# Attention with shared keys: the division by the softmax sums moved from the probabilities to the result

## The chip, the core and the metric

The kernel runs on one core of a Trainium2 chip as one program. The metric is its time on the device in microseconds (us). Five engines work side by side, each with its own queue of instructions that it takes in order: TensorE (PE; its weight loads are shown apart as PEld), VectorE (DVE), ScalarE (ACT), GpSimd (POOL), and SyncE (SP), which here issues all DMA transfers. Engines wait for each other through semaphores.

## The reference, cut to what matters

One layer of an encoder is applied to two requests that share the weights, a long one (1024 tokens) and a short one (512), each with 16 meta tokens ahead. Half of the mixer is grouped-query attention ("group A"): 8 query heads of width 64, four of which share one key and value head.

```
def gqa_block(qblk):
    s = jnp.einsum('bqhgd,bkhd->bhgqk', qblk, ka, preferred_element_type=jnp.float32) * scale
    p = jax.nn.softmax(s, axis=-1).astype(va.dtype)
    return jnp.einsum('bhgqk,bkhd->bqhgd', p, va)
```

`softmax` is exp(s - max) over its own sum along the keys. That division by the sum is what the change moves. The rest of the layer (projections, the differential attention of "group B", the output projection, a gated feed-forward part with a convolution, three norms) is computed as before.

## The kernel before, in words

All products are made in float32 precision: each operand is split into a high and a low part (function `split`, L114 on ACT for the high and L115 on DVE or POOL for the low part), and two or three matmuls are summed.

The program goes through these stages: the projections of the short request (`s = 1`); then the projections of the long request (`s = 0`) merged with the attention of the short one; then the attention of the long request merged with the output projection (`mixer_out`) and the feed-forward part (`conv_glu`) of the short one; then the rest for the long one. `merge` draws work from two generators by the sizes that they yield; behind it the framework's scheduler sets the order of the instructions on each engine, by its own estimate of times, so the order of a whole stage can shift when one operation goes.

Group A works in units: one head and 512 query positions. There are 8 units for the short and 16 for the long request, 24 in all. A unit has four softmaxes of 128 queries each. In `softmax`, scores come from TensorE chunk by chunk (L431, L432), DVE scales them into the tile `p` and takes the chunk's maximum (L433), DVE reduces the maxima (L436, `nm`), ACT makes the exponentials in place and their sum `l` (L438), DVE takes one over the sum (L442, `r`). Then DVE multiplies all of `p` by `r` (L508): 128 x 1040 numbers for the long request, 128 x 528 for the short one. `weighted_v` transposes the four `p` on TensorE, chunk by chunk of the keys (L456), splits the transposed chunk (L114, L115: `pt_hi`, `pt_lo`) and multiplies by the values (L470, L471, and L480 for the last 16 keys). Its result `o` has the output of the values' high parts in rows 0 to 63 and of their low parts in rows 64 to 127; `finish_a` copies the second half (L487, ACT) and adds it (L489, DVE: `o_a`), and SP sends `o_a` to scratch memory (`g.oT`, L514).

Two more things matter. `g.last_rows` holds the last two instructions of a softmax; the first four softmaxes of the long request are issued ahead, and `mixer_out` orders its splits behind those (`g.first_rows`). And SP issues everything in one queue: the loads of `q`, `k`, values and weights (`w_f`, L175), the stores to scratch, and the loads `m` of the attention's results in `mixer_out` (L608, three buffers).

Of the kernel before, what the change touches and what calls it, by code (L numbers as in the profile page):

```python
# [382 lines left out]
def attention(ctx, g, s, side):  # L383
# [40 lines left out]
    def softmax(q, k, inverse=True):  # L424
# [11 lines left out]
        nc.vector.tensor_reduce(out=nm, in_=mx[:, :nch], axis=AX.X, op=ALU.max, negate=True)  # L436
        l = sp.tile([P, 1], F32, name="l", tag="l")[:M]
        g.last_exp = nc.scalar.activation(p, p, AF.Exp, bias=nm, accum_out=l).ins  # L438
# [46 lines left out]
    def finish_a(o, W):  # L485
        low = op.tile([P, 512], F32, name="o_low", tag="w1", bufs=1)[:HD, :W]
        nc.scalar.copy(low, o[HD:P, :])  # L487
        oa = op.tile([P, 512], F32, name="o_a", tag="o")[:HD, :W]
        nc.vector.tensor_tensor(out=oa, in0=o[0:HD, :], in1=low, op=ALU.add)  # L489
        return oa  # L490

    nblk = N // 512
    for kv in range(2):
# [3 lines left out]
        for i in range(4):  # L497
            h = kv * 4 + i
            for b in range(nblk):
                off = 2 if b == 0 else 0  # L500
                q = load_q(QA + h // 2, h % 2, NMETA + 512 * b - off, 512 + off)
                if b == 0:
                    for f in range(2):
                        nc.gpsimd.tensor_copy(halo[f][:, 2 * i:2 * i + 2], q[f].bitcast(F32)[:, 0:2])
                pl = []
                for t in range(4):
                    p, _, r = softmax([x[:, off + t * P:off + (t + 1) * P] for x in q], k)
                    g.last_rows = [g.last_exp, nc.vector.tensor_scalar(  # L508
                        out=p, in0=p, scalar1=r, scalar2=None, op0=ALU.mult).ins]
# [49 lines left out]
    for h in range(4):  # L559
        ks = [load_k(KB + h, m) for m in range(2)]  # L560
        v = load_v(1 + h, 2 * P, 0)
        rows = g.oT[s][512 + h * P:512 + (h + 1) * P]
        for blk in blocks:
# [6 lines left out]
            nc.sync.dma_start(out=rows[:, c1:c1 + W - lead], in_=ob[:, lead:])  # L570
# [685 lines left out]
def trunk_kernel(ctx, tc, g):  # L1256
# [4 lines left out]
    g.qk, g.v, g.vt, g.oT = [], [], [], []  # L1261
    for s, N in enumerate(SEQS):
# [5 lines left out]
        g.oT.append(dram.tile([D, N + 1], F32, name=f"oT{s}"))  # L1268

# [157 lines left out]
```

## Time and profile before

| what | value |
|---|---|
| median of 3 runs | 2134.44 us (2131.06 to 2139.33) |
| the profiled execution: its own time | 2127.9 us |
| its span | 2126.1 us |
| granted TensorE clock, mean | 0.989 |
| PE / PEld busy | 96% / 86% of the span |
| DVE / ACT / POOL busy | 81% / 54% / 26% |

Matmuls are pipelined, so a PE that is shown as busy is not a PE at its peak; PEld and the number of matmuls in a stretch say more. Idle time of an engine costs only where the chain of waits runs through it. "Windows" are stretches of the span with the busy time of each engine in them; "groups" put together instructions of one line and shape. Times in the profile are those of one execution.

### The profile page before, as it was taken

How to read it: one execution, taken by the hardware profiler on the slowest of the kernel's cores; microseconds unless marked ns; L12 is line 12 of the kernel's file. 1: busy time of each engine (PE TensorE's matmuls, PEld its weight loads, DVE VectorE, ACT ScalarE, POOL GpSimd, SP SyncE). 2: the span in 40 equal slices, each digit the busy share in tenths (PEclk: the TensorE clock that was granted, in tenths of full speed). 3: DMA queues.
4: the chain of work that ended last, by engine and by line, in shares of the span. 5: the costliest groups of instructions: out<-in, count | busy, mean ns of one | idle time of the engine just before them, and what ended most of it. 6: DMA issues, size and time to landing. Idle time of an engine off the chain costs nothing.

```text
span 2126.1 us, 35236 instructions
## 1 busy us (share of the span) xinstructions
PE 2040.4 (96%) x12302; PEld 1822.3 (86%) x12302; DVE 1725.0 (81%) x3786; ACT 1156.0 (54%) x2253; POOL 560.8 (26%) x494
## 2 busy tenths in 40 slices
PE   6999999998999999999999999988999999999998
PEld 6988888997887989999989999987887777778877
DVE  6878889767879788888998885578778878879886
ACT  6635566544567556666666765345444444435454
POOL 4653233453112000000000000421544444330112
PEclk9999999999999999999999999999999999999999
DMA  7563435457621322223352225996322232247443
GB/s 255 176 203 130 119 111 171 153 178 236 209 79 56 105 75 67 74 82 118 104 187 88 86 97 147 276 290 217 107 100 90 101 113 84 94 167 260 119 126 127
DMA packets 171426, 296.31 MB, mean 139 GB/s; under 512 B 21456, under 2 KB 90608, under 8 KB 170736
## 3 DMA queue, kind: packets, MB, share of 16 engines
q1 hardware_dynamic: 171248, 294.05, 42.5%
q8 instruction: 97, 1.59, 0.3%
q14 instruction: 81, 0.66, 0.1%
HBM read 211.13 MB, written 82.85 MB: 138 GB/s over the span
## 4 chain that ended last, share of the span: by engine, by line
PE 76%; DVE 12%; DMA 4%; issue 3%; ACT 2%; POOL 1%; SPq 0%; DVEq 0%; ACTq 0%; POOLq 0%
PE ps_mm L121 17%; PE ps_mm L123 17%; PE ps_mm L122 17%; PE ps_t L456 5%; PE ps_s L431 3%; PE ps_s L432 3%; PE ps_s L122 2%; PE ps_s L123 2%; PE ps_s L121 2%; DVE p L433 2%; PE ps_o L471 2%; DVE w_lo L115 1%; PE ps_o L470 1%; DVE acc L972 1%; DMA m<-oT 1%
## 5 line engine op out<-in xcount | busy, mean ns | idle before, releaser
L121 PE MATMUL ps_mm<-xhi,w_hi 128*128 128x258 f32 (+3 forms) x1264 | 383.1, 303 | 12.3 <-ACT xhi L114 5.6
L122 PE MATMUL ps_mm<-xlo,w_hi 128*128 128x258 f32 (+3 forms) x1264 | 378.4, 300 | 0.3 <-POOL xlo L115 0.3
L123 PE MATMUL ps_mm<-xhi,w_lo 128*128 128x258 f32 (+3 forms) x1264 | 377.1, 299 | 0.3 <-DVE w_lo L115 0.3
L433 DVE TENSOR_SCALAR_CACHE_REDUCE p<-ps_s 114x344 f32<-114x344 f32 (+4 forms) x562 | 257.8, 489 | 28.1 <-PE ps_s L432 16.8
L114 ACT CAST pt_hi<-ps_t 128x512 fp32r<-128x512 f32 (+6 forms) x360 | 169.6, 484 | 180.8 <-PE ps_t L456 153.3
L121 PEld LDWEIGHTS ps_mm<-xhi,w_hi 128*128 128x128 f32 x1264 | 239.6, 190 | 18.3 <-ACT xhi L114 7.8
L438 ACT ACTIVATE p<-p,nm 114x1040 f32<-114x1040 f32 (+5 forms) x212 | 214.8, 1013 | 70.5 <-DVE nm L436 69.3
L115 DVE TENSOR_TENSOR w_lo<-w_f,w_hi 128x1024 fp32r<-128x1024 f32 (+1 forms) x182 | 195.2, 1080 | 67.3 <-ACT w_hi L114 66.8
L122 PEld LDWEIGHTS ps_mm<-xlo,w_hi 128*128 128x128 f32 x1264 | 240.0, 190 | 1.9 <-POOL xlo L115 0.8
L123 PEld LDWEIGHTS ps_mm<-xhi,w_lo 128*128 128x128 f32 x1264 | 239.4, 190 | 1.2 <-DVE w_lo L115 0.5
L114 ACT CAST w_hi<-w_f 128x1024 fp32r<-128x1024 f32 (+1 forms) x199 | 167.4, 856 | 79.3 <-PE ps_mm L122 52.2
L115 DVE TENSOR_TENSOR pt_lo<-ps_t,pt_hi 128x512 fp32r<-128x512 f32 (+4 forms) x312 | 172.0, 562 | 42.5 <-ACT pt_hi L114 40.9
L115 POOL TENSOR_TENSOR a_lo<-gate,a_hi 128x256 fp32r<-128x256 f32 x44 | 43.1, 981 | 540.9 <-ACT a_hi L114 521.0
L431 PE MATMUL ps_s<-k,q 128*114 128x348 f32 (+4 forms) x552 | 182.7, 336 | 3.2 <-DVE p L433 3.0
L456 PE MATMUL ps_t<-ident,p 128*128 128x128 f32 (+7 forms) x1188 | 182.4, 269 | 0.9 <-DVE nm L436 0.5
L121 PE MATMUL ps_s<-xhi,w_hi 128*128 128x256 f32 (+4 forms) x480 | 148.2, 311 | 23.2 <-DVE t L333 7.7
L432 PE MATMUL ps_s<-k,q 128*114 128x348 f32 (+4 forms) x552 | 170.3, 313 | 0.0
L456 PEld LDWEIGHTS ps_t<-ident,p 128*128 128x128 f32 (+7 forms) x1188 | 139.9, 135 | 29.1 <-issue 6.8
L123 PE MATMUL ps_s<-xhi,w_lo 128*128 128x256 f32 (+4 forms) x480 | 147.0, 307 | 3.2 <-DMA w_lo<-wo 3.0
L122 PE MATMUL ps_s<-xlo,w_hi 128*128 128x256 f32 (+4 forms) x480 | 148.7, 311 | 1.2 <-DVE xlo L115 0.5
L122 PE MATMUL ps_mm<-t_lo,w_hi 128*128 128x512 f32 (+2 forms) x368 | 142.8, 388 | 1.4 <-DVE t_lo L115 1.4
L121 PE MATMUL ps_mm<-t_hi,w_hi 128*128 128x512 f32 (+2 forms) x368 | 142.8, 388 | 0.0
(273 smaller groups left out, 5269.7 us busy)
## 6 DMA issues: line engine op xcount, KB each, us to landing
w_f<-w_gate SPq DMA_DIRECT2D x46, 512.0 KB, 3.4
w_f<-w_up SPq DMA_DIRECT2D x44, 512.0 KB, 3.3
w_f<-w_in SPq DMA_DIRECT2D x36, 512.0 KB, 4.0
a_f<-act SPq DMA_DIRECT2D x62, 256.0 KB, 2.7
w_f<-w_down SPq DMA_DIRECT2D x22, 512.0 KB, 3.4
act<-a_t SPq DMA_DIRECT2D x44, 256.0 KB, 2.1
a<-w_down SPq DMA_DIRECT2D x40, 256.0 KB, 5.4
w_hi<-wo SPq DMA_DIRECT2D x36, 256.0 KB, 5.2
```

The costliest lines, as they stand in the source:

```text
L114: return (nc.scalar.copy(hi, src).ins, (lo_engine or nc.vector).tensor_tensor(out=lo, in0=src, in1=hi.bitcast(F32), op=ALU.subtract).ins)
L115: (lo_engine or nc.vector).tensor_tensor(out=lo, in0=src, in1=hi.bitcast(F32), op=ALU.subtract).ins)
L121: nc.tensor.matmul(ps, lhsT=whi, rhs=xhi, start=start, stop=False)
L122: nc.tensor.matmul(ps, lhsT=whi, rhs=xlo, start=False, stop=False)
L123: return nc.tensor.matmul(ps, lhsT=wlo, rhs=xhi, start=False, stop=stop).ins
L431: nc.tensor.matmul(ps, lhsT=q[0], rhs=k[:, c0:c0 + cw], start=True, stop=False)
L432: nc.tensor.matmul(ps, lhsT=q[1], rhs=k[:, c0:c0 + cw], start=False, stop=True)
L433: nc.vector.tensor_scalar(out=p[:, c0:c0 + cw], in0=ps, scalar1=HD ** -0.5, scalar2=-3.0e38, op0=ALU.mult, op1=ALU.max, accum_out=mx[:, i: ...
L438: g.last_exp = nc.scalar.activation(p, p, AF.Exp, bias=nm, accum_out=l).ins
L456: nc.tensor.transpose(tps[:, c:c + M], p[:, k0:k0 + kw], g.ident[:M, :M])
L470: nc.tensor.matmul(o, lhsT=v[:, i, :], rhs=hi, start=i == 0, stop=False)
L471: nc.tensor.matmul(o, lhsT=v[:, i, :], rhs=lo, start=False, stop=False)
```

## The change

The values are multiplied by the exponentials as they are, and the result is divided. The sums of the four softmaxes of a unit go to one tile `l4` (128 x 4, two buffers). After the fourth softmax DVE takes one over all four columns at once; SP sends the tile to a row of 512 numbers in scratch memory (one per unit, `g.r`), and loads that row back, repeated on 64 partitions, into half of the tile `rows` (one buffer, whose two halves are used in turn). `finish_a` works in the same half, and GpSimd multiplies its result by `rows` before it is stored. L508 and three of each four reciprocals go. `g.last_rows` now names the maximum's reduction and the exponential, in `softmax` itself. The differential attention and the short "halo" softmaxes of group A keep their way. In the blocks of the differential attention a variable is renamed.

```diff
-    def softmax(q, k, inverse=True):
+    def softmax(q, k, inverse=True, l=None):
...
-        nc.vector.tensor_reduce(out=nm, in_=mx[:, :nch], axis=AX.X, op=ALU.max, negate=True)
-        l = sp.tile([P, 1], F32, name="l", tag="l")[:M]
-        g.last_exp = nc.scalar.activation(p, p, AF.Exp, bias=nm, accum_out=l).ins
+        most = nc.vector.tensor_reduce(out=nm, in_=mx[:, :nch], axis=AX.X, op=ALU.max, negate=True)
+        if l is None:
+            l = sp.tile([P, 1], F32, name="l", tag="l")[:M]
+        g.last_rows = [nc.scalar.activation(p, p, AF.Exp, bias=nm, accum_out=l).ins, most.ins]
...
-    def finish_a(o, W):
-        low = op.tile([P, 512], F32, name="o_low", tag="w1", bufs=1)[:HD, :W]
-        nc.scalar.copy(low, o[HD:P, :])
-        oa = op.tile([P, 512], F32, name="o_a", tag="o")[:HD, :W]
-        nc.vector.tensor_tensor(out=oa, in0=o[0:HD, :], in1=low, op=ALU.add)
+    def finish_a(o, W, half=slice(0, HD)):
+        other = slice(HD - half.start, P - half.start)
+        low = op.tile([P, 512], F32, name="o_low", tag="w1", bufs=1)[half, :W]
+        nc.scalar.copy(low, o[other])
+        oa = op.tile([P, 512], F32, name="o_a", tag="o")[half, :W]
+        nc.vector.tensor_tensor(out=oa, in0=o[half], in1=low, op=ALU.add)
         return oa
...
+    rows = op.tile([P, 512], F32, name="r_rows", tag="r_rows", bufs=1)
...
                 pl = []
+                l4 = sp.tile([P, 4], F32, name="l4", tag="l4", bufs=2)
                 for t in range(4):
-                    p, _, r = softmax([x[:, off + t * P:off + (t + 1) * P] for x in q], k)
-                    g.last_rows = [g.last_exp, nc.vector.tensor_scalar(
-                        out=p, in0=p, scalar1=r, scalar2=None, op0=ALU.mult).ins]
+                    p = softmax([x[:, off + t * P:off + (t + 1) * P] for x in q], k, False, l4[:, t:t + 1])[0]
                     pl.append(p)
+                    if t == 3:
+
+                        nc.vector.reciprocal(out=l4, in_=l4)
+                        row = g.r[s][h * nblk + b]
+                        nc.sync.dma_start(out=row.rearrange("(t p) -> p t", p=P), in_=l4)
+                        c = (h * nblk + b) % 2 * HD
+                        half = slice(c, c + HD)
+                        nc.sync.dma_start(out=rows[half], in_=row.unsqueeze(0).broadcast_to([HD, 512]))
                     yield 2 * n
                 o, W = yield from weighted_v(pl, v, False)
-                oa = finish_a(o, W)
+                oa = finish_a(o, W, half)
+                nc.gpsimd.tensor_tensor(out=oa, in0=oa, in1=rows[half], op=ALU.mult)
                 nc.sync.dma_start(out=g.oT[s][h * HD:(h + 1) * HD, 1 + 512 * b:513 + 512 * b], in_=oa)
...
+        g.r.append([dram.tile([512], F32, name=f"r{s}_{i}") for i in range(8 * N // 512)])
```

The scheduler moves instructions on every engine from the first unit of group A to the end of that attention. Three places are shown; line numbers of the change stand up to 13 higher than those of the kernel before.

DVE where the long request's attention begins, before; `p` and `mx` are a softmax's scores and maxima, `xlo` from `m` the first low parts of `mixer_out`, numbers tell buffers apart:

```order
L436 TENSOR_REDUCE nm_7262<-mx_7249 128x1
L433 TENSOR_SCALAR p_7308,mx_7309<-ps_s_7314 128x348
L442 RECIPROCAL r_6995<-l_6993 128x1
L433 TENSOR_SCALAR p_7308,mx_7309<-ps_s_7318 128x344
L433 TENSOR_SCALAR p_7329,mx_7330<-ps_s_7331 128x348
L508 TENSOR_SCALAR p_6977<-p_6977,r_6995 128x1040
L115 TENSOR_TENSOR xlo_6876<-m_7002,xhi_6875 128x258
```

The same place in the change:

```order
L436 TENSOR_REDUCE nm_7190<-mx_7177 128x1
L433 TENSOR_SCALAR p_7232,mx_7233<-ps_s_7238 128x348
L516 RECIPROCAL l4_6852<-l4_6852 128x4
L433 TENSOR_SCALAR p_7232,mx_7233<-ps_s_7242 128x344
L115 TENSOR_TENSOR xlo_6813<-m_6928,xhi_6812 128x258
```

The scaling is gone from between the chunks of scores, the first low part of `mixer_out` stands one chunk further ahead, and one reciprocal of four columns stands where one of four did.

PE at the change from the long request's projections to its attention, before; `ps_mm` are the projections, `ps_s` the scores:

```order
L121 MATMUL ps_mm_6829<-xhi7_1921,w_hi_6751 128x272
L122 MATMUL ps_mm_6829<-xlo7_1929,w_hi_6751 128x272
L123 MATMUL ps_mm_6829<-xhi7_1921,w_lo_6752 128x272
L431 MATMUL ps_s_6916<-k_6900,q_6908 128x348
L432 MATMUL ps_s_6916<-k_6900,q_6910 128x348
```

And the first scores of that attention in the change:

```order
L123 MATMUL ps_mm_6614<-xhi7_1943,w_lo_6575 128x384
L431 MATMUL ps_s_6855<-k_6838,q_6846 128x348
L432 MATMUL ps_s_6855<-k_6838,q_6848 128x348
L431 MATMUL ps_s_6859<-k_6838,q_6846 128x348
L432 MATMUL ps_s_6859<-k_6838,q_6848 128x348
L431 MATMUL ps_s_6863<-k_6838,q_6846 128x344
L432 MATMUL ps_s_6863<-k_6838,q_6848 128x344
L121 MATMUL ps_mm_6650<-xhi0_1936,w_hi_6574 128x272
```

Before, the last projection's matmul stood right ahead of the first scores. Now the scores of the first softmax stand ahead of the last four chunks of projections (96 matmuls), and part of those of the next among them.

SP in the change, at the long request's first unit; `r0_0` is the row in scratch memory, `r_rows` the tile that it is repeated into, `wo` a store of split weights:

```order
L518 DMA r0_0_80<-l4_6852 128x4x1
L620 DMA m_6941<-oT1_115 128x255
L620 DMA m_6946<-oT1_115 128x258
L620 DMA m_6950<-oT1_115 128x255
L521 DMA r_rows_6837<-r0_0_80 64x512
L630 DMA wo0_125<-w_hi_7002 128x1024
L402 DMA q_7924<-qk0_1_61 128x1x514
```

The row's store and its load are new in this queue; the load waits for the store to land, with stores, queries and weights queued behind it.

More of the change, by code (lines that the diff above doesn't have):

```diff
@@ L561, in attention @@
         v = load_v(1 + h, 2 * P, 0)
-        rows = g.oT[s][512 + h * P:512 + (h + 1) * P]
+        out = g.oT[s][512 + h * P:512 + (h + 1) * P]
         for blk in blocks:
```

4 lines of the change are left out of this document (2 added, 2 removed).

## The prediction

> **What bounds the kernel now.** I read the page first, then the chain of waits by stretches, then the windows of the stretches where group A runs. Two lines of the page: busy time, and the chain that ended last.
>
> ```profile
> PE 2040.4 (96%) x12302; PEld 1822.3 (86%) x12302; DVE 1725.0 (81%) x3786; ACT 1156.0 (54%) x2253; POOL 560.8 (26%) x494
> PE 76%; DVE 12%; DMA 4%; issue 3%; ACT 2%; POOL 1%; SPq 0%; DVEq 0%; ACTq 0%; POOLq 0%
> ```
>
> So TensorE sets the time over most of the span, and DVE over an eighth. What matters is whether the scalings (L508) lie in that eighth. The busy time of L508 alone, by windows that cover all of group A (no scaling runs from 345 to 500 us):
>
> ```profile
> core 0: us, DVE busy (x), PEclk, DMA share, GB/s
> 160.00:190.00 30.00, 5.12 (x8) 0.87 0.46 152
> 190.00:345.00 155.00, 15.62 (x24) 1.00 0.42 126
> 500.00:550.00 50.00, 7.57 (x10) 0.97 0.75 250
> 550.00:620.00 70.00, 8.78 (x11) 1.00 0.46 149
> 620.00:672.00 52.00, 7.07 (x9) 1.00 0.21 59
> 672.00:960.00 288.00, 26.09 (x34) 1.00 0.26 79
> sum 645.00, DVE 70.25; mean DVE 11.71
> ```
>
> All engines in three of them, and in the longest for comparison:
>
> ```profile
> core 0: us, PE busy (x) PEld busy (x) DVE busy (x) ACT busy (x) POOL busy (x), PEclk, DMA share, GB/s
> 160.00:190.00 30.00, 26.01 (x146) 23.61 (x146) 25.95 (x84) 16.05 (x37) 11.70 (x16) 0.87 0.46 152
> 500.00:550.00 50.00, 42.06 (x236) 33.59 (x235) 45.27 (x152) 30.43 (x58) 5.75 (x10) 0.97 0.75 250
> 620.00:672.00 52.00, 46.39 (x265) 35.28 (x264) 51.54 (x154) 37.47 (x76) 14.78 (x21) 1.00 0.21 59
> 672.00:960.00 288.00, 288.00 (x1951) 262.14 (x1951) 238.12 (x629) 174.93 (x293) 21.09 (x24) 1.00 0.26 79
> ```
>
> And the chain of waits in the same four, in order:
>
> ```profile
> by line: DVE p L433 14.5%; DVE p L508 11.4%; DVE t L321 7.6%; PE ps_mm L121 7.0%; PE ps_t L456 5.7%; ACT p L438 5.4%; PE ps_mm L122 5.1%; PE ps_mm L123 5.1%; PE ps_o L471 4.1%; DVE w L273 4.0%; DVE w L274 3.7%; DVE hn L106 3.5%; DVE hn L107
> by line: DMA m<-oT 29.1%; DVE p L433 20.3%; DMA q<-qk 10.8%; issue 5.3%; DVE w_lo L115 4.6%; DVE xlo L115 4.0%; ACT xhi L114 3.1%; PE ps_t L456 2.9%; DVE pt_lo L115 2.5%; PE ps_s L431 2.5%; DVE p L508 2.5%; PE ps_s L432 2.2%; POOL u L275 2.
> by line: DVE p L433 24.2%; DVE pt_lo L115 15.2%; DVE p L508 8.4%; DVE t L761 8.2%; issue 5.7%; DVE pt_hi L115 3.9%; POOL xlo L115 3.4%; ACT pt_hi L114 3.2%; PE ps_t L456 3.0%; DVE w_lo L115 2.8%; DVE o_a L489 2.3%; PE ps_o L470 2.3%; ACT w_
> by line: PE ps_mm L121 18.9%; PE ps_mm L122 18.7%; PE ps_mm L123 18.5%; PE ps_t L456 14.3%; PE ps_s L431 7.5%; PE ps_s L432 7.3%; PE ps_o L471 6.8%; PE ps_o L470 6.5%; PE ps_o L480 1.5%
> ```
>
> From 672 to 960 us the chain never leaves TensorE: the 26.1 us of scalings there cost nothing, and their removal brings nothing. In the three short stretches DVE is the bound: when the short request's first units meet the projections; when the long request's attention starts beside `mixer_out`; and when `conv_glu` normalises its input, where DVE is busy 51.5 of 52 us. What TensorE loses there bounds any gain: at the weight-load share of the longest stretch (262.14 of 288, 0.91) the three would show 27.3, 45.5 and 47.3 us instead of 23.6, 33.6 and 35.3, so 3.7 + 11.9 + 12.0 = 27.6 us.
>
> **What is removed.** All 96 scalings, 70.25 us of DVE, and 72 of 96 reciprocals. The reciprocals in the three stretches:
>
> ```profile
> 160.00:190.00 30.00, 1.32 (x9) 0.87 0.46 152
> 500.00:550.00 50.00, 1.59 (x10) 0.97 0.75 250
> 620.00:672.00 52.00, 1.46 (x10) 1.00 0.21 59
> ```
>
> The chain's own shares of L508 are 0.114 x 30 = 3.4, 0.025 x 50 = 1.3 and 0.084 x 52 = 4.4 us, 9.1 us together: the gain if nothing else moves. If each microsecond of DVE work in the three counted, it would be 5.1 + 7.6 + 7.1 = 19.8 us of scalings and three quarters of 4.4 us of reciprocals, 23 us. I take, stretch by stretch: the first 4 us, its chain share and half of its reciprocals. The last 6 us, between 4.4 and 8.2, since DVE has no gap there but TensorE and ACT take over parts of the chain. The middle one 4 us, between 1.3 and 8.8: four scalings stand in an unbroken run of DVE work ahead of the first low parts of `mixer_out`, and the order now puts the scores of the first softmax ahead of four chunks of projections, so that TensorE has work where it had 236 matmuls in 50 us. In the other three windows I take nothing. The longest is TensorE's alone, and the other two nearly so:
>
> ```profile
> 190.00:345.00 155.00, 151.44 (x971) 136.32 (x970) 133.51 (x428) 94.82 (x223) 47.73 (x42) 1.00 0.42 126
> 550.00:620.00 70.00, 69.98 (x526) 65.98 (x525) 52.58 (x143) 38.48 (x68) 13.07 (x15) 1.00 0.46 149
> ```
>
> Weight loads take 0.88 and 0.94 of them, against 0.91 in the longest. If that cover were gone, they would add at most their 15.6 and 8.8 us of scalings. Sum of the gains: 14 us.
>
> **What is added.** GpSimd multiplies 64 x 512 numbers 24 times. Its nearest groups:
>
> ```profile
> L115 POOL TENSOR_TENSOR a_lo<-gate,a_hi 128x256 fp32r<-128x256 f32 x44 | 43.1, 981 | 540.9 <-ACT a_hi L114 521.0 <-issue 15.7 <-ACT pt_hi L114 2.9
> L910 POOL TENSOR_TENSOR w_s<-w_f 128x512 f32<-128x512 f32 x31 | 52.9, 1707 | 72.7 <-DVE w_lo L115 58.7 <-issue 13.2
> L1017 POOL TENSOR_TENSOR a_t<-act 128x512 f32<-128x512 f32 x22 | 28.4, 1290 | 27.3 <-DMA act<-act 23.6 <-DVE act L1009 3.7
> ```
>
> Half the columns take 0.98 us, as many take 1.29 to 1.71; I take 1.4 us, 34 us in all, beside a GpSimd that is busy 7% to 39% of the windows above. The result's PSUM buffer is free again before the multiply, and its store is needed only in the next stage. Behind the multiply on GpSimd stand the rotary products of the projections in the short request's units, and the low parts `xlo` of `conv_glu` from 620 us on, for which TensorE does wait; there the order puts two multiplies among sixteen splits, up to 2.8 us. I take 1 us.
>
> The row goes out as 512 single numbers and comes back as 64 rows of 2 KB (128 KB). The nearest transfers, with KB each and the median time to landing last:
>
> ```profile
> oT<-o_a SPq DMA_DIRECT2D x16, 0.2 KB, 1.8
> m<-oT SPq DMA_DIRECT2D x8, 0.5 KB, 2.5
> m<-oT SPq DMA_DIRECT2D x8, 172.0 KB, 5.6
> yT<-y SPq DMA_DIRECT2D x32, 128.0 KB, 1.9
> oT<-o_a SPq DMA_DIRECT2D x24, 128.0 KB, 3.0
> ```
>
> 64 numbers land in 1.8 us, 128 in 2.5; the slowest kind of `m` load takes 5.6 (172 KB). I put the row at 3 us (between 1.8 and 5.6) and its load at 3 us (1.9 to 3.4). Their 6 us are hidden if the result comes later. Fourth scaling and result of the long request's first unit, from the timeline:
>
> ```profile
> 517.55 0.76 DVE L508 TENSOR_SCALAR p<-p,r 128x1040 f32<-128x1040 f32 x1
> ...
> 546.64 0.68 DVE L489 TENSOR_TENSOR o_a<-ps_o,o_low 64x512 f32<-64x512 f32 x1
> ```
>
> That is 29 us, so the row waits for the result, not the other way. What isn't hidden is SP: the row's load waits for its store to land, and for those 3 us nothing behind it is issued. In the second stretch the chain runs through such loads in series:
>
> ```profile
> 526.05 7.00 DMA m<-oT
> 533.97 4.48 DMA m<-oT
> 539.42 3.08 DMA m<-oT
> ```
>
> One row's 3 us falls among them with some of it on the path; I take 1 us (nothing to 5.6). The 23 other waits I put at nothing: the transfers behind them are queries, weights and stores that were asked for ahead. If that cover were gone, each would cost 1.8 to 5.6 us.
>
> Net: 14 - 1 - 1 = 12 us less. The profiled execution took 2127.9 us (span 2126.1), so 2115.9. It stands 6.5 us under the median of the runs, 2134.4; the same step gives **2122 us**.
>
> **A rule against it.** The splits of weights on DVE read two operands from SBUF, those of the transposed chunks one from PSUM:
>
> ```profile
> L115 DVE TENSOR_TENSOR pt_lo<-ps_t,pt_hi 128x512 fp32r<-128x512 f32 x160 | 107.7, 683 | 25.2 <-ACT pt_hi L114 24.2
> L115 DVE TENSOR_TENSOR w_lo<-w_s,w_hi 128x512 fp32r<-128x512 f32 x106 | 95.4, 900 | 43.4 <-ACT w_hi L114 43.4
> L508 DVE TENSOR_SCALAR p<-p,r x96: 474/754/2298, 166.0 to 897.6; 128x1040 f32<-128x1040 f32 x64, 128x528 f32<-128x528 f32 x32
> ```
>
> The second group runs in a later stage beside a busy GpSimd and takes 0.22 us more for the same shape; one scaling took 2.30 us where the shortest took 0.47 (minimum, median and maximum in the third row). The Trainium skill (SBUF — State Buffer, section "Who interferes with whom") says that a DVE instruction with two SBUF inputs, or one in a two-port mode such as `tensor_scalar`, and a GpSimd instruction that reads SBUF lock each other out for a whole instruction. By that page the removed scalings were such holders and the added multiplies are such holders too. The rows agree in direction.
>
> **Rivals.** *Locked out by GpSimd:* the multiplies hold up DVE's two-input work where DVE is the bound. The stretches hold 8 + 10 + 9 = 27 of the 96 scalings, so about 7 of 24 units; 7 x 1.4 = 10 us would take all but 2 us of the gain: 2132. For it: 0.90 against 0.68 us. Against: most of DVE's work in those stretches reads PSUM (L433, `pt_lo`). Chance 0.05.
>
> *Hidden anyway:* the DVE-bound stretches are bound by the scores' eviction (L433 has 1.3 to eight times L508's share), and the new order gives back what is won; the gain is 4 us at most: 2130. For it: L508 is only 2.5% of the middle chain. Against: 11.4% and 8.4% in the others. Chance 0.20; that the change acts on paper only is the same case.
>
> *SP stands still (the slower side):* each row's store holds the queue. At 5.6 us, three units in the middle stretch lose 17 us, and the short request's eight, whose `q` loads and stores stand right behind, 2.5 us each, 20 us. All of it less the 12 would be 25 us slower; half of the losses, 18.5 less 12, still 6.5 us slower: 2141 to 2159; I take 2148. It decides once a row takes over 4 us to land with a load behind it that is needed at once: three such waits are 12 us. For it: `m` loads are 29% of the middle chain. Against: the chain from 672 us on is free of DMA. Chance 0.13.
>
> *More than the sum:* the order of the middle stretch closes its loss (11.9 us) as well, and the other two give all they hold, 5.1 + 8.2: 25 us, 2109. Chance 0.12. The forecast has 0.50.
>
> **How the numbers follow.** About 0.5% (10.7 us) is what a measurement of this kernel can tell from no change: below 2123.8 is faster, above 2145.1 slower. The forecast's own range is 2113 to 2129, two thirds of it below 2123.8: 0.33, and 0.12 of the larger gain: 0.45 faster. Slower: 0.12 from SP, and 0.04 for an order that goes wrong elsewhere: 0.16. The rest, 0.39, is no change. The range for 8 in 10 leaves out the far halves of the larger gain and of SP's loss: 2105 to 2145.
>
> **What would show it.** Right: in the three stretches DVE's share falls and the matmuls in 50 us rise; L508's place on the chain is empty; GpSimd gains 30 to 40 us; 672 to 960 keeps its length. Wrong: SP waiting on the row's store with loads late behind it; `xlo` or `rope` products waiting behind the multiply; L433 taking over the whole share; or stretches without group A changing length, which would be the order and not the work.

## The result: 1.5% slower, and the profile after

The kernel with the change takes 2166.0 us (median of 4 runs, 2163.9 to 2166.6) against 2133.9 us before (2131.1 to 2139.3). The ratio is 1.0154, with a 95% interval of 1.0131 to 1.0177: slower by 32 us, outside the predicted range of 2105 to 2145 us. The profiled execution took 2166.2 us (span 2164.4 us), 38.3 us more than that of before.

Busy time and the chain that ended last, from the page of the kernel after:

```profile
PE 2062.0 (95%) x12302; PEld 1845.8 (85%) x12302; DVE 1672.0 (77%) x3618; ACT 1154.0 (53%) x2254; POOL 588.8 (27%) x518
PE 74%; DVE 12%; DMA 7%; issue 3%; ACT 3%; POOL 1%; SPq 0%; DVEq 0%; ACTq 0%; POOLq 0%
```

DVE lost 53 us of work as planned (1725.0 before), GpSimd gained 28, and TensorE ran the same 12,302 matmuls. What grew on the chain is DMA, from 4% to 7% of the span. The two new transfers, in the list of DMA issues of the same page (KB each, median us from issue to landing), and the store's extremes from the view of its line:

```profile
r_rows<-r SPq DMA_DIRECT2D x24, 128.0 KB, 3.7
r<-l SPq DMA_DIRECT2D x24, 2.0 KB, 8.6
```

```profile
L518 SPq DMA_DIRECT2D r<-l x24: 371/383/832, 172.5 to 912.2; - x24
...
DMA to landing us min/median/max: 7.7/8.6/11.9
```

The load lands in 3.7 us, near the 3 us forecast. The store of 2 KB lands in 8.6 us and never in less than 7.7, where the prediction had 3 us and an upper bound of 5.6. The trace holds the landings of 11 of the 24 stores and of 11 of the 24 loads; the waits of the DMA queue from 150 to 1000 us (us in total, times, longest) cover all 24 stores, and 206.9 / 24 is 8.6 us too. SP stands for each of them:

```profile
SPq L521 <- DMA r<-l: 206.9, 24, 11.4
SPq L402 <- PE ps_s L432: 80.3, 29, 8.5
```

All engines in the windows of the prediction, with 345 to 500 us added:

```profile
core 0: us, PE busy (x) PEld busy (x) DVE busy (x) ACT busy (x) POOL busy (x), PEclk, DMA share, GB/s
160.00:190.00 30.00, 27.70 (x173) 24.46 (x171) 22.26 (x75) 16.20 (x37) 8.99 (x13) 1.00 0.71 128
190.00:345.00 155.00, 140.87 (x858) 127.04 (x858) 115.97 (x348) 88.67 (x208) 51.44 (x47) 0.93 0.43 122
345.00:500.00 155.00, 148.56 (x980) 144.69 (x980) 109.52 (x317) 77.79 (x197) 70.33 (x59) 0.97 0.49 159
500.00:550.00 50.00, 45.33 (x257) 40.41 (x256) 32.16 (x104) 21.73 (x42) 16.52 (x22) 0.93 0.68 213
550.00:620.00 70.00, 55.85 (x364) 50.10 (x364) 39.87 (x114) 32.59 (x62) 8.16 (x10) 0.90 0.68 178
620.00:672.00 52.00, 51.18 (x358) 45.95 (x356) 39.18 (x113) 32.01 (x58) 10.83 (x12) 1.00 0.33 88
672.00:960.00 288.00, 284.80 (x1886) 253.94 (x1886) 222.56 (x592) 180.51 (x309) 45.08 (x50) 1.00 0.30 81
```

The one window of before that the prediction does not show:

```profile
345.00:500.00 155.00, 150.89 (x1006) 147.38 (x1005) 108.11 (x298) 75.37 (x189) 75.47 (x64) 0.99 0.50 163
```

Count the matmuls. In the three stretches that DVE set before, there are more of them: 173, 257 and 358 against 146, 236 and 265. In the windows that the prediction put at nothing there are fewer: 858 against 971, 364 against 526, 1886 against 1951. At the pace of the longest window before (1951 in 288 us, 6.8 per us), 162 fewer in 550 to 620 us are 24 us and 113 fewer in 190 to 345 us are 17 us. (Work has moved between neighbouring windows, so single rows tell the place and not a price.) Over all seven windows the change has 225 fewer, 33 us at that pace, and the last scores of the long request start 29.9 us later than before (1283.3 against 1253.4 us). So most of the 38 us is lost in this part of the execution. The chain of waits from 500 to 620 us, in part, in order of time from 542 us:

```profile
542.59 5.94 DMA wo<-w_hi
548.59 13.03 DMA m<-oT
...
570.63 3.00 DMA m<-oT
...
575.89 9.18 DMA r<-l
585.09 0.48 SPq L521
585.66 4.00 DMA res<-xT
```

A load of `m` that takes 13 us; then a row's store of 9.2 us, SP issuing the row's load behind it, and only then the load of `res` for which `mixer_out` waits. In the chain of before from 500 to 620 us, no DMA is longer than 7.0 us.

The granted clock fell too, in these two executions from 0.989 to 0.975 as a mean over the span: 0.025 x 2164.4 = 54 us of TensorE's full speed withheld, against 23 us. The last section returns to it.

### The profile page after: what moved, and what is told of

Same layout as the page of the kernel before. It is cut to its first block, busy times and chain, and to the rows that moved or that the text cites. A ratio compares the mean times of both kernels' runs of the same rounds, so it can differ in the third digit from the quotient of the medians.

```text
span 2164.4 us, 35271 instructions
## 1 busy us (share of the span) xinstructions
PE 2062.0 (95%) x12302; PEld 1845.8 (85%) x12302; DVE 1672.0 (77%) x3618; ACT 1154.0 (53%) x2254; POOL 588.8 (27%) x518
## 4 chain that ended last, share of the span: by engine, by line
PE 74%; DVE 12%; DMA 7%; issue 3%; ACT 3%; POOL 1%; SPq 0%; DVEq 0%; ACTq 0%; POOLq 0%
PE ps_mm L121 17%; PE ps_mm L123 17%; PE ps_mm L122 17%; PE ps_t L457 5%; PE ps_s L431 3%; PE ps_s L432 3%; PE ps_s L123 2%; PE ps_s L122 2%; PE ps_s L121 2%; DVE w_lo L115 2%; DMA m<-oT 2%; PE ps_o L472 1%; PE ps_o L471 1%; DVE p L433 1%; DVE acc L984 1%
## 5 line engine op out<-in xcount | busy, mean ns | idle before, releaser
L433 DVE TENSOR_SCALAR_CACHE_REDUCE p<-ps_s 114x344 f32<-114x344 f32 (+4 forms) x562 | 258.7, 489 | 50.0 <-PE ps_s L432 33.2
L431 PE MATMUL ps_s<-k,q 128*114 128x348 f32 (+4 forms) x552 | 184.9, 340 | 10.2 <-DVE p L433 5.3
```

The lines of the kernel that those rows point to most:

```text
L431: nc.tensor.matmul(ps, lhsT=q[0], rhs=k[:, c0:c0 + cw], start=True, stop=False)
L433: nc.vector.tensor_scalar(out=p[:, c0:c0 + cw], in0=ps, scalar1=HD ** -0.5, scalar2=-3.0e38, op0=ALU.mult, op1=ALU.max, accum_out=mx[:, i: ...
```

## The experiments

Fifteen kernels were run, each beside the kernel before on the same chip. Three theories stood at the start. A: SP stands still for the row's store, and what is queued behind it comes late. B: the order of instructions that the change brings costs the time. C: the transfers or GpSimd's multiply cost it by themselves.

| kernel | what it has in place of the scalings | us, median | ratio to before, 95% |
|---|---|---|---|
| the change | 512 single numbers stored, row loaded, multiply on GpSimd | 2166.0 | 1.0154 [1.0131, 1.0177] |
| `e1_other_row` | the same, but the load waits for no store | 2159.7 | 1.0142 [1.0122, 1.0163] |
| `e2_runs_of_four` | 128 pieces of 16 bytes | 2133.2 | 1.0006 [0.9991, 1.0022] |
| `e3_no_division` | nothing | 2117.0 | 0.9939 [0.9916, 0.9962] |
| `e4_transfers_alone` | scalings kept, both transfers added | 2161.3 | 1.0156 [1.0126, 1.0187] |
| `e5_runs_of_two` | 256 pieces of 8 bytes | 2133.9 | 1.0008 [0.9988, 1.0029] |
| `e6_store_act_queue` | as e1, store issued by ScalarE | 2153.9 | 1.0111 [1.0077, 1.0145] |
| `e7_late_load` | as e2, load written later | 2132.3 | 1.0002 [0.9986, 1.0018] |
| `e8_diagonal` | product with a diagonal matrix, no row | 2206.0 | 1.0351 [1.0325, 1.0377] |
| `e9_one_half` | as e2, load behind the multiply before | 2130.8 | 0.9993 [0.9978, 1.0008] |
| `e10_multiply_alone` | multiply, no transfers | 2127.1 | 0.9974 [0.9957, 0.9991] |
| `e11_apart` | as e1, the 512 numbers 64 bytes apart | 2127.2 | 0.9984 [0.9968, 0.9999] |
| `e12_scale_on_act` | scalings on ScalarE | 2140.0 | 1.0042 [1.0024, 1.0059] |
| `e13_where_it_pays` | as e2 in 7 units, scalings in 17 | 2133.0 | 1.0000 [0.9986, 1.0014] |
| `e14_stretches_alone` | nothing in 7 units, scalings in 17 | 2125.0 | 0.9968 [0.9951, 0.9985] |
| `e15_multiply_on_dve` | as e9, multiply on VectorE | 2140.6 | 1.0036 [1.0022, 1.0050] |

`e1_other_row`, `e3_no_division`, `e6_store_act_queue`, `e10_multiply_alone`, `e11_apart` and, in 7 units, `e14_stretches_alone` leave out the division by the sums; the others compute the whole result. "Before" is the kernel before in the executions of the same round, and the ratio is the one to go by across rounds.

### First round: is it SP, the order or the transfers?

**e1_other_row** takes away what the load waits for:

```diff
-nc.sync.dma_start(out=rows[half], in_=row.unsqueeze(0).broadcast_to([HD, 512]))
+nc.sync.dma_start(out=rows[half], in_=g.xT[s][0:1, 0:512].broadcast_to([HD, 512]))
```

> The change, but the row that SP loads back is a row of an input and not the one just stored, so SP issues the same two transfers and waits for neither; this leaves out the division by the sums. Theory A (SP stands still: in the profile of the change SP waits 207 us for the rows' stores to land, 24 times 8.6 us, with loads queued behind): the loss goes, 2110 to 2135 us. Theory B (the scheduler's new order costs the time, not the wait): still 2155 us or more. Theory C (the transfers or GpSimd's multiply themselves cost it): 2150 us or more.

It took 2159.7 us. So SP's standing as such is not what costs: without it the loss is all but the same, and theory A falls in the form in which it stood. What took its place is seen in one window, 172 to 182 us, in which the first row is stored (at 172.5 us in the change, 173.9 in e1). The first fence is the kernel before, the second the change, the third e1_other_row, each row with the last three columns clock, DMA share and GB/s:

```profile
172.00:182.00 10.00, 7.06 (x39) 5.67 (x37) 9.88 (x29) 5.33 (x14) 5.43 (x7) 0.98 0.28 93
```

```profile
172.00:182.00 10.00, 9.10 (x51) 6.92 (x50) 9.81 (x29) 7.16 (x17) 5.51 (x7) 1.00 1.00 30
```

```profile
172.00:182.00 10.00, 9.17 (x51) 7.24 (x49) 9.81 (x24) 6.64 (x15) 6.37 (x8) 1.00 0.90 30
```

Before, the 16 transfer engines were busy 28% of these 10 us and moved 93 GB/s. With a row in it they are busy 90 to 100% and move 30 GB/s. The row's own 512 packets are recorded 0.9 to 1.2 us behind its issue; what fills the time after them are the packets of the load of weights that is issued next, of which the slowest takes 9.5 us in the change, and that load lands after 12.8 us. So whatever comes behind the row's writes is held. In the change SP keeps the other transfers back by standing, in e1 it issues them and they lie in the engines. By the list of DMA issues of e1:

```profile
q<-qk SPq DMA_DIRECT2D x32, 257.0 KB, 9.3
v<-v SPq DMA_DIRECT2D x17, 256.0 KB, 9.3
r<-l SPq DMA_DIRECT2D x24, 2.0 KB, 9.8
```

The same queries and values before:

```profile
q<-qk SPq DMA_DIRECT2D x32, 257.0 KB, 3.9
v<-v SPq DMA_DIRECT2D x17, 256.0 KB, 3.3
```

The trace of e1 holds few of these landings (two of the queries, one of the values, one of the 24 stores; all of those before), so its three medians show that such landings occur and not how often.

**e2_runs_of_four** stores the same 2 KB as 128 pieces of 16 bytes. The row is then in another order, which the multiply undoes:

```diff
-nc.sync.dma_start(out=row.rearrange("(t p) -> p t", p=P), in_=l4)
+nc.sync.dma_start(out=row.rearrange("(p t) -> p t", t=4), in_=l4)
-nc.gpsimd.tensor_tensor(out=oa, in0=oa, in1=rows[half], op=ALU.mult)
+view = oa.rearrange("c (t p) -> c t p", t=4)
+nc.gpsimd.tensor_tensor(out=view, in0=view, in1=rows[half].rearrange("c (p t) -> c t p", t=4), op=ALU.mult)
```

> The change, but the row is stored as 128 runs of 16 bytes in place of 512 single numbers, and GpSimd's multiply reads it with a stride. Theory A: the store lands in 2 to 4 us instead of 8.6, SP waits under 100 us instead of 207, 2125 to 2150 us. Theory B and C: no change, 2160 to 2170 us, GpSimd's multiply as long or longer.

It took 2133.2 us: 1.5% of the time back, level with before. The store's landing and SP's wait for it:

```profile
DMA to landing us min/median/max: 1.4/2.5/6.3
```

```profile
SPq L521 <- DMA r<-l: 42.2, 23, 4.1
```

So the whole of the loss against before goes with the way in which 2 KB are cut up.

**e3_no_division** leaves out reciprocals, transfers and multiply (its result is not divided by the sums):

```diff
-nc.vector.reciprocal(out=l4, in_=l4)
-nc.sync.dma_start(out=row.rearrange("(t p) -> p t", p=P), in_=l4)
-nc.sync.dma_start(out=rows[half], in_=row.unsqueeze(0).broadcast_to([HD, 512]))
-nc.gpsimd.tensor_tensor(out=oa, in0=oa, in1=rows[half], op=ALU.mult)
```

> The change without one over the sums, without both transfers and without the multiply: what taking the scalings off VectorE is worth by itself; this leaves out the division by the sums. Theory A: the gain that was forecast, 2110 to 2128 us. Theory B: the order without scalings is the slow one, 2150 us or more. Theory C: as A.

It took 2117.0 us, 13.8 less than the 2130.8 of before in that round; by the ratio 13 us, with an interval of 8 to 18. That is the predicted gain of 14 us, and it speaks against theory B: an order without the scalings is the fastest of all. Its windows:

```profile
160.00:190.00 30.00, 28.90 (x168) 25.62 (x167) 23.24 (x69) 16.06 (x38) 11.46 (x17) 0.95 0.48 157
190.00:345.00 155.00, 147.60 (x949) 133.00 (x948) 122.41 (x389) 95.53 (x226) 45.31 (x41) 0.99 0.40 125
500.00:550.00 50.00, 43.53 (x258) 35.96 (x257) 39.78 (x141) 33.61 (x66) 5.22 (x8) 0.97 0.69 235
550.00:620.00 70.00, 70.00 (x526) 66.13 (x525) 48.43 (x132) 40.05 (x70) 12.51 (x16) 1.00 0.47 152
620.00:672.00 52.00, 50.04 (x315) 41.00 (x314) 46.75 (x134) 38.72 (x79) 12.43 (x21) 1.00 0.20 58
672.00:960.00 288.00, 288.00 (x1948) 262.91 (x1947) 221.03 (x594) 178.00 (x302) 22.39 (x24) 1.00 0.27 85
```

Against before: 22 more matmuls in the first stretch, 22 in the second, 50 in the third; 22 fewer from 190 to 345 us; the same within three in the rest. At 6.8 per us, that is 3.2, 3.2 and 7.4 us, where the prediction had 4, 4 and 6.

**e4_transfers_alone** is the kernel before, with its scalings, plus the store of 512 numbers and the load, whose row nobody reads.

> The kernel before, all scalings kept, with the two transfers of the change added (the sums themselves stored as 512 single numbers and loaded back on 64 partitions, and not used). Theory A: the wait of SP alone makes it slower than before, 2150 to 2185 us. Theory B: 2126 to 2142 us, as before. Theory C: between, by what the transfers load the queues.

It took 2161.3 us, 30.5 more than before. Theory B is out for most of the loss: here the scalings stand as before. By itself the run fits theory A as well as the transfers of theory C, since SP waits here for the rows too (204.1 us). With e1, where SP does not wait and the loss is the same, it is the transfers, and GpSimd's multiply isn't needed for it.

### Second round: what makes the store slow?

**e5_runs_of_two** cuts the row into 256 pieces of 8 bytes:

```diff
-nc.sync.dma_start(out=row.rearrange("(t p) -> p t", p=P), in_=l4)
+nc.sync.dma_start(out=row.rearrange("(a p t) -> p a t", a=2, t=2), in_=l4.rearrange("p (a t) -> p a t", a=2))
```

> The row goes out as 256 pieces of two numbers (8 bytes) in place of 512 of one; the multiply reads it in the matching order, so the output is complete. The first four runs left this: with 512 pieces a row takes 8.6 us to land and the kernel 2160 to 2166 us, with 128 pieces of 16 bytes 2.5 us and 2133 us. Theory D (what is slow grows with the number of small pieces): a landing of about 4.5 us, by a straight line between the two, and 2138 to 2150 us. Rival (only a write of a single number is slow): a landing of about 2.5 us and 2130 to 2136 us.

It took 2133.9 us, as with 128 pieces, though the landing is longer:

```profile
DMA to landing us min/median/max: 2.7/3.9/8.8
```

(Its multiply undoes the order in two halves.) The best landings of 128, 256 and 512 pieces are 1.4, 2.7 and 7.7 us: the last doubling adds four times as much as the one before. Theory D came near the landing (4.5 us expected) and had the time wrong; the rival had the time. A landing of 4 us, at which SP stands 76 us in all, costs the kernel no more than one of 2.5 us.

**e6_store_act_queue** is e1 with the store on ScalarE's queue:

```diff
-nc.sync.dma_start(out=row.rearrange("(t p) -> p t", p=P), in_=l4)
+nc.scalar.dma_start(out=row.rearrange("(t p) -> p t", p=P), in_=l4)
```

> As e1_other_row (the load reads a row of the input, so the division by the sums is left out and nothing waits for the store), but the store of 512 single numbers is issued by ScalarE, on its own queue. e1_other_row took 2159.7 us with the store on SyncE's queue, and behind a store the packets of the next transfer there took up to 5.4 us each in place of 0.16 us. Theory D (the writes hold the 16 transfer engines, whoever issued them): 2150 to 2165 us, and packets of SyncE's transfers still slow behind a store. Theory E (the writes hold only the queue that issued them): 2120 to 2138 us, packets of SyncE's transfers at their usual time.

It took 2153.9 us. Its interval overlaps that of e1, so a small part may belong to the queue, but most of the loss stays. SP's transfers are still held: from 150 to 950 us the trace has 131 packets of 1 KB or more that take over 3 us, against 161 in e1 (the slowest there 9.3 us, more than the 5.4 of the expectation) and none before. So the writes hold the transfer engines although ScalarE issued them, and another queue is no way out.

**e11_apart** is e1 with every number 64 bytes from the next, in a scratch of 512 x 16:

```diff
-nc.sync.dma_start(out=row.rearrange("(t p) -> p t", p=P), in_=l4)
+nc.sync.dma_start(out=row.rearrange("(t p) w -> p t w", p=P)[:, :, 0], in_=l4)
```

> As e1_other_row (division by the sums left out, nothing waits for the store), but the 512 numbers of a row are written 64 bytes apart in the scratch. e1_other_row took 2159.7 us. If each write of four bytes is slow by itself: 2150 to 2165 us, packets behind a store as slow as there. If the writes are slow because neighbours share the same few lines of memory: 2118 to 2138 us, packets behind a store at their usual time.

It took 2127.2 us, 32 us less than e1 with the same 512 pieces of four bytes, the same issue and the same packets (recorded 0.9 to 1.2 us behind the issue here too). Landing, and the window 172 to 182 us:

```profile
DMA to landing us min/median/max: 1.8/2.4/5.9
```

```profile
172.00:182.00 10.00, 9.10 (x51) 7.03 (x50) 9.81 (x28) 6.83 (x16) 6.06 (x9) 1.00 0.50 144
```

All 24 landings are in this trace. The load of weights behind the first row lands after 4.1 us, not 12.8, and no packet of 1 KB or more takes over 3 us. So neither the number of the pieces nor their size alone makes them slow, and with the same instructions as e1 in the same order theory B is out. It is single numbers written *next to each other*: they land in 8.6 us in the change, the same writes spread out in 2.4 us. This is the experiment that names the cause. (It is no version to keep: its row would have to be read in 512 pieces by each of 64 partitions. That was not tried.)

### Third round: the rest of the gain

With the store mended, the kernel is level with before; 16 us lie between `e2_runs_of_four` and `e3_no_division`, for which the prediction had 2.

**e7_late_load** writes the row's load behind the products with the values, directly ahead of the multiply.

> As e2_runs_of_four, with the row's load issued behind the unit's products with the values, directly ahead of the multiply, in place of directly behind the store; the output is complete. e2_runs_of_four took 2133.2 us against 2117.0 us of e3_no_division, and SyncE stood 42 us for the stores in it. If this standing is what is left of the loss: 2118 to 2127 us. If it is the transfers themselves, GpSimd's multiply and the order that they bring: 2129 to 2137 us.

It took 2132.3 us, but did not test what it meant to: the scheduler left the load in its place, and SP's wait (41.8 us, 22 times) is that of e2. **e9_one_half** enforces it with a real dependency, the same 64 partitions for every row:

```diff
-c = (h * nblk + b) % 2 * HD
+c = 0
```

> As e2_runs_of_four (128 pieces of 16 bytes), but every row is loaded into the same 64 partitions, so a row's load comes behind the multiply of the unit before it and stands later on SyncE's queue, by when its store has landed; the output is complete. e7_late_load, which only wrote the load later, left it in its place on the queue: SyncE stood 42 us for the stores there as in e2_runs_of_four. e2_runs_of_four took 2133.2 us, e3_no_division, with nothing in place of the scalings, 2117.0 us. If the standing for the store is what takes the 16 us: 2118 to 2126 us, with under 15 us of standing for stores. If it is the traffic or the multiply, or if SyncE now stands for the multiply: 2129 to 2140 us.

SP's wait for the rows' stores falls to 4.7 us in two places; the time is 2130.8 us, 0.1% below e2, with intervals that overlap. Standing 42 us in pieces of 2 us costs nothing that can be measured, as the prediction had it for the 23 other waits. The 16 us are elsewhere.

**e10_multiply_alone** keeps GpSimd's multiply and drops reciprocals and rows; it multiplies by a row of the input, loaded once:

```diff
-nc.sync.dma_start(out=rows[half], in_=row.unsqueeze(0).broadcast_to([HD, 512]))
+nc.sync.dma_start(out=rows, in_=g.xT[s][0:P, 0:512])   # once, ahead of the loops
```

> As e3_no_division (no reciprocal, no row stored or loaded), with GpSimd's multiply of every result kept: the row is one of the input, loaded once, so the division by the sums is left out. It tells the multiply apart from the transfers in the 16 us between e3_no_division (2117.0 us) and e2_runs_of_four (2133.2 us). If the multiplies are hidden, as the prediction put them (1 us): 2114 to 2121 us, and the 16 us belong to the transfers. If they cost it: 2127 to 2136 us.

It took 2127.1 us. Between the ratios of e10 and e3 lie 0.0035, 7.5 us (the two intervals together leave 1.3 to 13.6), and from e10 to e2 another 0.0032, 6.8 us (2 to 12), for rows, reciprocals and a multiply that reads with a stride (1.56 us instead of 1.29). The time lies at the lower edge of what the second hypothesis allowed (2127 to 2136 us), but the difference is about half of the 16 us and not all of it. It does not arise where the multiplies run. In the profiles, e10 is 13.8 us longer than e3, but the last scores of the long request start 2 us *earlier* (1237.9 against 1240.0 us; 1253.4 before). The difference arises behind them, where neither kernel has a multiply: the last `t_lo` on DVE starts 5 us later than in e3 (1458.2 against 1453.0 us), and then comes this. TensorE in e10, and then in e3 (5 us and more ahead, so the rows hold different matmuls):

```profile
1450.00:1460.00 10.00, 7.81 (x61) 0.97 0.95 342
1460.00:1470.00 10.00, 10.00 (x44) 0.50 0.01 2
1470.00:1480.00 10.00, 10.00 (x38) 0.85 0.17 54
```

```profile
1450.00:1460.00 10.00, 9.86 (x77) 1.00 0.58 186
1460.00:1470.00 10.00, 10.00 (x45) 1.00 0.16 54
```

In e10 TensorE stood 22% of the 10 us at the end of a stretch full of transfers, and then ran at half clock for 13.7 us, 6.8 us of full speed withheld. The change (17.1 us from 1498 us on), e1, e2 and e6 show the same; e3 and the kernel before do not. But the spell does not go with the multiply: e4_transfers_alone and e12_scale_on_act, which have no such multiply, show it (13.7 us each), and e5_runs_of_two and e9_one_half, which have all 24, do not. Each kernel has one profiled execution. So what the multiplies by themselves cost, and how, isn't shown; a different meeting of loads in that stretch is the nearest guess.

**e15_multiply_on_dve** asks whether it is GpSimd:

```diff
-nc.gpsimd.tensor_tensor(out=view, in0=view, ...)
+nc.vector.tensor_tensor(out=view, in0=view, ...)
```

> As e9_one_half (2130.8 us), with the 24 multiplies moved from GpSimd (1.3 us each) to VectorE; the output is complete. If it is GpSimd's work, late behind its other operations, that costs the 7 us of e10_multiply_alone: 2122 to 2128 us. If the order and the transfers cost it, or VectorE lacks the room: 2129 to 2136 us.

It took 2140.6 us, 0.4% more than e9. GpSimd was the better place.

**e14_stretches_alone** and **e13_where_it_pays** test the places of the gain. Only 7 of the 24 units do without scalings, with nothing in their place in e14 and with rows of 16-byte pieces in e13:

```diff
+here = h * nblk + b in ((0, 1, 5, 6, 7) if s == 0 else (0, 1))
 for t in range(4):
+    if here: p = softmax(..., False, l4[:, t:t + 1])[0]
+    else: p, _, r = softmax(...); p scaled on VectorE as before
```

> Only the scalings of those 7 units are left out, with nothing in their place (their division by the sums is left out); the other 17 units scale on VectorE as before. The prediction's places, tested by themselves: if the three stretches hold the gain, 2116 to 2122 us, as e3_no_division with 2117.0 us. If it is spread over all 24 units, 7 of them give 4 us: 2126 to 2130 us.

> As e2_runs_of_four, but only 7 of the 24 units send a row and multiply their result: the first two of the shorter sequence and units 0, 1, 5, 6 and 7 of the longer one, which lie in the three stretches that the prediction named; the other 17 scale their probabilities on VectorE as before. The output is complete. If the gain of 13.8 us (e3_no_division) sits in these stretches and the price of rows and multiplies (16 us for 24 units) goes by their number, 7 units cost 5 us: 2121 to 2127 us. If the gain is spread over all units: 2128 to 2136 us.

e14 took 2125.0 us: by the ratio 6.8 us (3 to 10), half of e3's gain from 29% of the units, between the two forecasts. An even spread over all units would give 3.8 us, which lies within the interval, and the whole gain of 13 us lies outside it. So these seven units do not seem to hold it all, and that they hold more than their share isn't shown. e13 took 2133.0 us, no different from before: rows and multiplies in seven units use up what they bring.

**e8_diagonal** and **e12_scale_on_act** do without any row.

```diff
-nc.tensor.transpose(tps[:, c:c + M], p[:, k0:k0 + kw], g.ident[:M, :M])
+nc.tensor.matmul(tps[:, c:c + M], lhsT=p[:, k0:k0 + kw], rhs=by[j], start=True, stop=True)   # by[j]: 1/sum on the diagonal
```

> The kernel before without the scalings, and without any row: ScalarE writes a 128x128 matrix with one over the sums on its diagonal (96 copies), and the transposes of these heads become products with that matrix, so that the result comes out divided; the output is complete. From the trace of before: a product of 114x114 by a diagonal matrix took 273 ns where a transpose of that size took 260 ns, so 736 of them cost TensorE at most 10 us beside the 13.8 us that the scalings were worth: 2118 to 2130 us. Rival: the weight loads (192 ns in place of 141 ns) and the 96 copies of about 0.39 us on ScalarE come onto the path: 2135 to 2160 us.

```diff
-nc.vector.tensor_scalar(out=p, in0=p, scalar1=r, scalar2=None, op0=ALU.mult)
+nc.scalar.activation(p, p, AF.Copy, scale=r)
```

> The kernel before with the 96 scalings moved from VectorE to ScalarE and nothing else; the output is complete and no row is sent. ScalarE is busy 54% of the span, VectorE 81%; the scalings were worth 13.8 us on VectorE (e3_no_division). If ScalarE has the room where VectorE sets the pace: 2117 to 2127 us. If the scaling, some 1.2 us beside an exponential of 1.2 us, makes ScalarE late with the casts of the transposed tiles: 2132 to 2155 us.

e8 took 2206.0 us. Its expectation misread a row: each of these products runs as two matmuls, so 736 transposes became 1472 instructions, 1280 of them in this group, which had 640 before:

```profile
L457 PE MATMUL ps_t<-e,p 128*128 128x128 f32 x1280 | 180.6, 279 | 0.0
```

736 more at about 0.28 us issue partly overlapped; TensorE's busy time rises by 88 us (2128.5 against 2040.4) and the kernel by 74. e12 took 2140.0 us, 0.4% more than before: a scaling takes 1.16 us on ScalarE against 0.75 on VectorE (medians). That it comes between the exponentials and the casts of the transposed tiles is the likely reason, and not tested.

No version was found that beats the kernel before with its whole result. The nearest, `e9_one_half`, is level with it.

## Why the prediction was wrong, step by step

**The step that failed is the price of the row's store: "I put the row at 3 us (between 1.8 and 5.6)".** It lands in 8.6 us, outside the bounds. They came from the store of 64 single numbers (1.8 us) and from loads; by the kernel's code those 64 go into a column of `oT`, each into another row, a few KB apart. Taken as the nearest row by number and size of the pieces, it was the wrong neighbour in the one respect that decides: e11_apart, whose numbers also stand apart, lands 512 of them in 2.4 us.

**The second part of the same step is that the other 23 waits were put at nothing.** For waits of 2 to 4 us this holds (e2, e5, e9). For 8.6 us it does not, and the reason is not SP alone: while the writes go on, the transfer engines are held (e1, e6), so transfers asked for "ahead" are late as well. The cover named in the prediction, loads issued early, is no cover when the engines that carry them are held. Both transfers alone cost 30.5 us (e4_transfers_alone), against 1 us in the sum.

**The slower rival** had the sign, the place (the `m` loads of the middle stretch) and the point from which it decides: "once a row takes over 4 us to land with a load behind it". Its time, 2141 to 2159 us, stopped short of 2166. Its mechanism, SP standing, is only one of the two forms: e1_other_row has no such wait and is as slow. Its chance of 0.13 was too low because the bounds of the store left only their upper end for it.

**What was right.** The removal: 14 us forecast, 13.8 measured by the medians (e3), 13.0 by the ratio (8 to 18); in the profile of e3 the three stretches show it almost in the forecast's shares, and 13.4 us of it are there by the last scores of the long request. That the sum agrees to within a microsecond is luck, with an interval of 10 us. The places are supported by these windows and not proved, since seven units alone bring half of it (e14). The longest window keeps its 288 us of TensorE in e3, as forecast. SP's short waits: nothing, as forecast.

**What was wrong in size.** The multiply: the single one takes 1.3 us (1.4 forecast), but the kernel with 24 of them is 7.5 us slower (1.3 to 13.6) and not 1, in a later stage and in a way that stays open (e10). Rows of 16-byte pieces, reciprocals and the strided multiply come with 6.8 us more. The sum from the runs, in ratios to before: 13.0 us gained by the removal; 7.5 lost with the multiply; 6.8 with rows in a good form; 31.6 more with single numbers side by side. That makes 32.9 us slower. (The terms are steps from one ratio to the next, so they add up by construction; each has its own interval.)

**The other rivals.** *Locked out by GpSimd* finds no support: the eviction of the scores (L433) takes 489 ns on average before and after, the low parts `pt_lo` 562 and 564 ns. Both read PSUM; of the work with two inputs from SBUF, of which the rival speaks, the largest group from 160 to 960 us (`w_lo`, 128 x 1024) takes 1239 ns before, 1221 in the change and 1254 in e10. *Hidden anyway* is disproved by e3. *More than the sum* did not come in any run.

**The signs that it named.** L508 has left the chain, and DVE's work in the three stretches fell from 123 to 94 us while the matmuls there rose from 647 to 788; GpSimd gained 28 us, just under the 30 to 40. From 672 to 960 us, which was to keep its length, TensorE lost 65 matmuls in the change and three in e3. And of the signs against it, the first one named is what happened: "SP waiting on the row's store with loads late behind it".

## What to carry to other kernels

When a transfer has no counterpart in the trace, compare the pieces' places in memory too, not only their number and size: 512 numbers written side by side took 8.6 us in the median and 12 at most, where the same numbers apart, or in pieces of 8 or 16 bytes, took 2.4 to 3.9. A tile with a few numbers per partition should be stored so that each partition writes them as a run, and the reader should undo the order; here runs of two were enough. A slow transfer is not hidden by issuing the others early when it holds the engines that all of them use: a DMA share near 1.00 beside 30 GB/s is such a hold.

## What the hardware showed that was not expected

**Neighbouring four-byte writes hold all transfer engines.** 24 stores of 2 KB, 48 KB in all, cost 30 us, with the loads of the rows (e4). Where nothing else was in the way, the trace has the packets of such a store 0.9 to 1.2 us behind its issue; the landing comes over 6 us later, and the engines get little else done until then (1.00 busy at 30 GB/s). From 150 to 950 us, packets of 1 KB or more that take over 3 us number 53 in the change, 55 in e4, 161 in e1 and 131 in e6; 12 in e5; none before, in e2 and in e11. The Trainium skill ("DMA: Bandwidth & Descriptors", section "Specifications") says that a transfer below 512 bytes makes the engine read, modify and write. That would fit writes that wait for each other in one place, but by its threshold pieces of 8 and 16 bytes side by side should suffer as much, and they cost the kernel nothing measurable (e2, e5); four bytes alone and apart don't suffer either (e11). Where the line runs between 4 and 8 bytes, and whether it is the 64 bytes that matter or less, no run here shows. The same page (section "Back-pressure in remote DMA") says, of transfers to another core, that stalled writes stall the other queues of their engine; e6_store_act_queue agrees for a store to the device's memory, 1.1% slower with the store on a queue of its own.

**Half clock comes in spells of 3.4 us, and they grow with the loss.** In the profiles the granted clock is either full or half. Half comes in spells of 3.4, 6.8, 10.2, 13.7 or 17.1 us, all of them multiples of 3.4: eight before, 41 us in all, and 19 in the change, 102 us (the end of the execution left aside). The Trainium skill ("TensorE: Matmul & The Clock Gate", section 'Part 1: The HAM clock gate (the "warmup" mystery)') gives half clock after an idle window of about 3.4 us until one busy window has passed. The trace agrees with the length of the window, but not with the end of every spell: from 1498 to 1515 us in the change TensorE was 99% busy and stayed at half clock for five such lengths.

Over all executions the mean clock is 0.975 in the change (0.975 to 0.978), 0.978 in e4 and 0.979 in e1, against 0.986 before (0.985 to 0.989 in the first round) and 0.988 in e3. So the change has some 24 us more withheld (0.025 x 2164 less 0.014 x 2126). How much of the loss this makes is not shown: e2 has 0.983 at the time of before. That the spells follow from the waits is argued from their place and not tested. No term of the prediction had this, and a stall on a path that TensorE sets should be priced with it.
